# Token and position embedding on one core: the positions loaded in one DMA, two sequences with direct indices, natural order of the gathers

## The chip, the cores and the metric

The kernel runs on one core of a Trainium2 chip. The time is the device time of one execution in microseconds; a comparison uses several runs of each kernel on the same chip. Beside the times there is a profile of one execution, with every engine instruction and every DMA packet.

The engines that matter here: GpSimd (POOL in the profile) issues the gathers, VectorE (DVE) adds, ScalarE (ACT) copies, TensorE (PE) transposes the index table, and SyncE (SP) issues the plain loads and the stores. All transfers run on 16 DMA engines.

## The reference

```python
batch, seq_len, vocab_size, d_model = 32, 512, 50000, 512
def reference(indices, embedding_table, position_embed):
    token_embed = embedding_table[indices]
    return (token_embed + position_embed).astype(np.float32)
```

Indices are 64-bit when they reach the chip (32 x 512 of them), the table is 50,000 rows of 512 float32 (2 KB a row), the positions are 512 rows of 2 KB (1 MB), and the output is 32 x 512 rows of 2 KB (33.55 MB). So 33.55 MB of rows are gathered, the same number of bytes is stored, and 1 MB of positions and 0.14 MB of indices are loaded beside them.

## The kernel before

A sequence has 512 = 128 x 4 rows. Partition p holds rows 4p to 4p+3 of a sequence; the four are called k = 0 to 3. One gather fetches one k of one sequence b: 128 rows, one per partition, 256 KB, into the slot of that sequence. There are 23 slots in SBUF (`slots`), each for a whole sequence, so that sequence 23 takes the slot of sequence 0 again. In all there are 32 x 4 = 128 gathers, 128 adds (`tensor_tensor`, one per gather) and 68 stores, most of them of two k at once (512 KB, 4 KB a partition).

Nothing is scheduled by a planner: each engine's instructions are written out in order, with semaphores between them. The list `order` (lines 73 to 75) gives the order of gathers on POOL and of adds on VectorE, which is the same; the list `stores` (76 to 81) gives the stores on SP. A gather is numbered g by its place in `order`, from 0. Before, the first 16 gathers run in two halves: k = 0 and 1 of the first four sequences (`FIRST = 4`), then k = 2 and 3 of the same four; the rest goes sequence by sequence.

The gathers need an index per partition. For the first `FIRST` sequences the indices are loaded directly (`idx0`, lines 105 and 109), with 32 B pieces: sequence 0 in one DMA, sequences 1 to 3 in a second. For the others the whole index array is loaded in long rows (`idx_raw`, line 113), cast to float (164), transposed on TensorE in four steps (154), and cast back into `idx_t` by four VectorE casts (170). These casts stand on VectorE between the adds of gathers, at places that `g == 7` (the first cast) and `g == 9` (the last four) set. POOL waits for `idx_t` before gather `FIRST * K`, which is gather 16 (line 133).

The positions come in four DMAs of 256 KB, one per k (`load_pos`, line 98), on SP: k = 0 and k = 1 among the index loads, k = 2 when k = 1 has landed (116), k = 3 when the first gather has landed (118). ScalarE copies each k from `pos_sb` in SBUF to `pos_ps` in PSUM (182), and all 128 adds read `pos_ps`; in sequence 0 an add waits for the copy of its k (174).

On SP the stores (191) stand behind the loads; each waits for the count of adds it needs. On POOL a gather g waits for gather g - 16 to have landed (148), and the first gather of a sequence from 23 on waits for the stores of the slot's last user (137).

Of the kernel before, what the change touches and what calls it, by code (L numbers as in the profile page):

```python
# [8 lines left out]
K = 4  # L9
SLOTS = 23  # L10
LANES = 16
FIRST = 4
Q = 32


# [1 line left out]
def kernel(  # L17
# [64 lines left out]

    sem = tc.alloc_semaphore
    s_first, s_next, s_raw = sem("s_first"), sem("s_next"), sem("s_raw")
    s_pos = [sem(f"s_pos{k}") for k in range(K)]
# [8 lines left out]
    def rounds(g):  # L94
        return 16 * (g // LANES + 1)

    def load_pos(engine, k):
        engine.dma_start(out=pos_sb[:, k, :], in_=pos_rows[:, k, :]).then_inc(
            s_pos[k], 16
        )  # L100

    with tc.tile_critical(no_gpsimd_drain=True):  # L102


        nc.sync.dma_start(out=idx0[:, 0, :], in_=idx_first[:, 0, :]).then_inc(
            s_first, 16
        )
        load_pos(nc.sync, 0)
        nc.sync.dma_start(out=idx0[:, 1:, :], in_=idx_first[:, 1:, :]).then_inc(
            s_next, 16  # L110
        )
        load_pos(nc.sync, 1)
        nc.sync.dma_start(
            out=idx_raw[:], in_=idx_rows.rearrange("r (s w) -> r s w", w=2)
        ).then_inc(s_raw, 16)
        nc.sync.wait_ge(s_pos[half - 1], 16)
        load_pos(nc.sync, half)
        nc.sync.wait_ge(s_gather[0], 16)
        load_pos(nc.sync, half + 1)


        nc.gpsimd.memset(ones[:], 1.0).then_inc(s_ident, 1)  # L122
# [1 line left out]
            out=ident[:], in_=ones[:], pattern=[[-1, P]],  # L124
# [2 lines left out]
        )._wait_ge(s_ident, 1).then_inc(s_ident, 1)  # L127
        nc.gpsimd.wait_ge(s_first, 16)
        for g, (b, k) in enumerate(order):
            if g == half:  # L130
                nc.gpsimd.wait_ge(s_next, 16)
            if g == FIRST * K:
                nc.gpsimd.wait_ge(s_idx, J)
            if b >= SLOTS and k == 0:
                done = sum(1 for x in stores if x[1] == b - SLOTS)
                nc.gpsimd.wait_ge(s_out[b - SLOTS], 16 * done)
            if b < FIRST:
                where = idx0[:, b, 2 * k : 2 * k + 1]
            else:
                where = idx_t[:, k, b : b + 1]  # L140
            ins = nc.gpsimd.indirect_dma_start(  # L141
                out=slots[b % SLOTS][:, k, :],
                out_offset=None,
                in_=table,
                in_offset=bass.IndirectOffsetOnAxis(ap=where, axis=0),
            ).then_inc(s_gather[g % LANES], 16)
            if g >= LANES:
                ins._wait_ge(s_gather[g % LANES], rounds(g - LANES))
# [11 lines left out]


        for g, (b, k) in enumerate(order):
            if g == 7:
                nc.vector.tensor_copy(  # L164
                    out=idx_f[:].rearrange("r p k -> r (p k)"), in_=idx_raw[:, :, 0]
                )._wait_ge(s_raw, 16).then_inc(s_cast, 1)
            if g == 9:
                nc.vector.wait_ge(s_turn, K)
                for j in range(J):
                    nc.vector.tensor_copy(  # L170
                        out=idx_t[j * Q : (j + 1) * Q, :, :], in_=turned[:, :, :, j]
                    ).then_inc(s_idx, 1)
            if b == 0:
                nc.vector.wait_ge(s_ps, k + 1)
            part = slots[b % SLOTS][:, k, :]
            nc.vector.tensor_tensor(  # L176
                out=part, in0=part, in1=pos_ps[:, k, :], op=add
            )._wait_ge(s_gather[g % LANES], rounds(g)).then_inc(s_add, 1)


        for k in range(K):
            nc.scalar.copy(out=pos_ps[:, k, :], in_=pos_sb[:, k, :])._wait_ge(  # L182
                s_pos[k], 16
            ).then_inc(s_ps, 1)


# [1 line left out]
        for adds, b, at, n in stores:  # L188
# [3 lines left out]
                out=out_rows[b][:, at : at + n, :],  # L192
                in_=slots[b % SLOTS][:, at : at + n, :],
# [32 lines left out]
```

## Time and profile before

| | before |
|---|---|
| median of 5 runs | 183.41 us (183.33 to 183.49) |
| the profiled execution's own time | 183.44 us |
| its span in the profile | 182.2 us |
| POOL busy, instructions | 122.2 us (67%), 134 |
| VectorE busy, instructions | 89.0 us (49%), 133 |
| ScalarE busy | 3.6 us |
| TensorE busy | 1.0 us |
| read from HBM, written to HBM | 34.75 MB, 33.55 MB |
| mean traffic over the span | 375 GB/s |

The span runs from the first to the last recorded event of the program; the time has 1.24 us around it. [...] A DMA share of an engine stretch can be a little above 1, since packets overlap at their ends. A line number (L141) is that of the kernel above. In the timeline, what stands in brackets is the idle time before an instruction and what ended it.

### The profile page before, as it was taken

To read this page: it belongs to the slowest core of one execution; us is meant where nothing else is said; L and a number is where in the kernel's file an instruction comes from. 1 tells how busy PE (TensorE), PEld (TensorE's weight loads), DVE (VectorE), ACT (ScalarE), POOL (GpSimd) and SP (SyncE) were. 2 spreads that over 40 slices of the span, in tenths; PEclk is the share of its full clock that TensorE was granted. 3 is DMA by queue.
4 is the path that set the end of the run, shared out by engine and by line. 5 is a ranking of instruction groups with operands and counts; after the bars stand their busy time and mean duration, and the time that the engine had idled before them with its cause. 6 is when DMAs were issued, how large, how long until landed. Compare 5 with 4: busy or idle time off the path is not lost.

```text
span 182.2 us, 427 instructions
## 1 busy us (share of the span) xinstructions
PE 1.0 (1%) x4; PEld 0.4 (0%) x4; DVE 89.0 (49%) x133; ACT 3.6 (2%) x5; POOL 122.2 (67%) x134
## 2 busy tenths in 40 slices
PE   0002000000000000000000000000000000000000
PEld 0000000000000000000000000000000000000000
DVE  0137646446544455555555545645556555556300
ACT  2220000000000000000000000000000000000000
POOL 4777777777777777777777777777777777760000
DMA  3899999999999999999999999999999999999900
GB/s 99 237 354 369 345 401 397 399 410 413 402 412 415 405 418 418 416 412 406 401 406 416 421 420 418 420 418 417 420 419 419 421 418 420 417 419 418 361 6 0
DMA packets 21299, 68.34 MB, mean 375 GB/s; under 512 B 3760, under 2 KB 3888, under 8 KB 21296
## 3 DMA queue, kind: packets, MB, share of 16 engines
q0 software_dynamic: 10240, 33.56, 47.4%
q1 hardware_dynamic: 11056, 34.76, 47.4%
q14 instruction: 3, 0.02, 0.0%
HBM read 34.75 MB, written 33.55 MB: 375 GB/s over the span
## 4 chain that ended last, share of the span: by engine, by line
POOL 63%; issue 23%; DMA 5%; DVE 2%; POOLq 1%; SPq 0%
POOL slot L141 63%; DMA slot<-in_embedding_table_dram,idx_t 5%; DVE slot L176 2%; DMA idx<-in_indices_dram 1%; POOLq L149 1%; SPq L221 0%; SPq L102 0%
## 5 line engine op out<-in xcount | busy, mean ns | idle before, releaser
L141 POOL DMA_INDIRECT slot<-in_embedding_table_dram,idx_t x112 | 106.2, 948 | 34.1 <-issue 34.1
L176 DVE TENSOR_TENSOR slot<-slot,pos_ps 128x512 f32<-128x512 f32 x128 | 87.8, 688 | 81.9 <-issue 51.0
L141 POOL DMA_INDIRECT slot<-in_embedding_table_dram,idx x16 | 15.4, 960 | 5.9 <-issue 4.6
L182 ACT COPY pos_ps<-pos_sb 128x512 f32<-128x512 f32 x4 | 2.4, 589 | 8.0 <-DMA pos_sb<-in_position_embed_dram 8.0
L182 ACT ACT_TABLE_LOAD x1 | 1.3, 1283 | 1.0 <-SPq L102 1.0
L170 DVE CAST idx_t<-turned 32x128 int32<-32x128 f32 x4 | 1.1, 280 | 0.1
L154 PE MATMUL turned<-ident,idx_f 128*32 128x128 f32 x4 | 1.0, 413 | 16.7 <-issue 16.7
L122 POOL MEMSET ones<- 128x128 f32 x1 | 0.2, 205 | 0.5 <-SPq L102 0.5
L154 PEld LDWEIGHTS turned<-ident,idx_f 128*32 128x32 f32 x4 | 0.4, 131 | 16.8 <-issue 16.7
L123 POOL TENSOR_SCALAR_AFFINE_SELECT ident<-ones 128x128 f32<-128x128 f32 x1 | 0.3, 289 | 0.1
L210 POOL MEMSET const-float32-0.0<- 128x1 f32 x1 | 0.1, 101 | 0.3 <-issue 0.3
L164 DVE CAST idx_f<-idx_raw 128x128 f32<-128x128 int32 x1 | 0.2, 220 | 0.0
L210 POOL MEMSET const-uint8-127<- 128x1 uint8 x1 | 0.1, 118 | 0.0
L210 POOL MEMSET const-bfloat16-1.0<- 128x1 bf16 x1 | 0.1, 112 | 0.0
L210 POOL MEMSET const-float32-1.0<- 128x1 f32 x1 | 0.1, 103 | 0.0
## 6 DMA issues: line engine op xcount, KB each, us to landing
out_dram<-slot SPq DMA_DIRECT2D x60, 512.0 KB
out_dram<-slot SPq DMA_DIRECT2D x8, 256.0 KB
slot<-in_embedding_table_dram,idx_t POOLq DMA_INDIRECT x112
pos_sb<-in_position_embed_dram SPq DMA_DIRECT2D x4, 256.0 KB, 3.0
slot<-in_embedding_table_dram,idx POOLq DMA_INDIRECT x16
idx_raw<-in_indices_dram SPq DMA_DIRECT2D x1, 128.0 KB
idx<-in_indices_dram SPq DMA_DIRECT2D x1, 4.0 KB, 1.6
idx<-in_indices_dram SPq DMA_DIRECT2D x1, 12.0 KB, 3.0
```

What stands on the lines that cost most here:

```text
L122: nc.gpsimd.memset(ones[:], 1.0).then_inc(s_ident, 1)
L123: nc.gpsimd.affine_select(out=ident[:], in_=ones[:], pattern=[[-1, P]], compare_op=mybir.AluOpType.is_equal, fill=0.0, base=0, channel_mul ...
L141: ins = nc.gpsimd.indirect_dma_start(out=slots[b % SLOTS][:, k, :], out_offset=None, in_=table, in_offset=bass.IndirectOffsetOnAxis(ap=whe ...
L149: nc.gpsimd.drain()
L154: ins = nc.tensor.transpose(turned[:, k].rearrange("p b j -> p (b j)"), idx_f[:, :, k], ident[:])
L164: nc.vector.tensor_copy(out=idx_f[:].rearrange("r p k -> r (p k)"), in_=idx_raw[:, :, 0])._wait_ge(s_raw, 16).then_inc(s_cast, 1)
L170: nc.vector.tensor_copy(out=idx_t[j * Q : (j + 1) * Q, :, :], in_=turned[:, :, :, j]).then_inc(s_idx, 1)
L176: nc.vector.tensor_tensor(out=part, in0=part, in1=pos_ps[:, k, :], op=add)._wait_ge(s_gather[g % LANES], rounds(g)).then_inc(s_add, 1)
L182: nc.scalar.copy(out=pos_ps[:, k, :], in_=pos_sb[:, k, :])._wait_ge(s_pos[k], 16).then_inc(s_ps, 1)
L210: nc = _bacc.Bacc("TRN2", target_bir_lowering=False, num_devices=1)
```

## The change

`FIRST` becomes 2, and the indices of these two sequences come in one DMA. The gathers run in natural order, sequence by sequence and k by k. The positions come in one DMA of 1 MB, whose descriptors are 8 KB (all four k of a partition), issued directly after the first indices, with one semaphore. The four adds of sequence 0 read the positions from SBUF (`pos_sb`) and wait for that DMA; all other adds read the copy in PSUM (`pos_ps`), and those of sequence 1 wait for the copies. The index table's first cast now stands before the add of gather 2, its four last casts before the add of gather 4, and POOL waits for the table before gather 8. Only k = 0 and 1 of sequence 0 are stored one by one; those of sequence 1 are stored as a pair.

```diff
-FIRST = 4
+FIRST = 2
...
-    order = [(b, k) for h in range(2) for b in range(FIRST)
-             for k in range(h * half, (h + 1) * half)]
-    order += [(b, k) for b in range(FIRST, B) for k in range(K)]
+    order = [(b, k) for b in range(B) for k in range(K)]
     stores = []
     for g, (b, k) in enumerate(order):
-        if (b <= 1 and k < half) or b == B - 1:
+        if (b == 0 and k < half) or b == B - 1:
...
-        nc.sync.dma_start(out=idx0[:, 0, :], in_=idx_first[:, 0, :]).then_inc(
-            s_first, 16
-        )
-        load_pos(nc.sync, 0)
-        nc.sync.dma_start(out=idx0[:, 1:, :], in_=idx_first[:, 1:, :]).then_inc(
-            s_next, 16
-        )
-        load_pos(nc.sync, 1)
+        nc.sync.dma_start(out=idx0[:], in_=idx_first).then_inc(s_first, 16)
+        nc.sync.dma_start(out=pos_sb[:], in_=pos_rows).then_inc(s_pos, 16)
         nc.sync.dma_start(
             out=idx_raw[:], in_=idx_rows.rearrange("r (s w) -> r s w", w=2)
         ).then_inc(s_raw, 16)
-        nc.sync.wait_ge(s_pos[half - 1], 16)
-        load_pos(nc.sync, half)
-        nc.sync.wait_ge(s_gather[0], 16)
-        load_pos(nc.sync, half + 1)
...
         for g, (b, k) in enumerate(order):
-            if g == half:
-                nc.gpsimd.wait_ge(s_next, 16)
             if g == FIRST * K:
                 nc.gpsimd.wait_ge(s_idx, J)
...
-            if g == 7:
+            if g == 2:
                 nc.vector.tensor_copy(
                     out=idx_f[:].rearrange("r p k -> r (p k)"), in_=idx_raw[:, :, 0]
                 )._wait_ge(s_raw, 16).then_inc(s_cast, 1)
-            if g == 9:
+            if g == 4:
                 nc.vector.wait_ge(s_turn, K)
...
-            if b == 0:
+            if g == 0:
+                nc.vector.wait_ge(s_pos, 16)
+            if b == 1:
                 nc.vector.wait_ge(s_ps, k + 1)
+            pos = pos_sb if b == 0 else pos_ps
             part = slots[b % SLOTS][:, k, :]
             nc.vector.tensor_tensor(
-                out=part, in0=part, in1=pos_ps[:, k, :], op=add
+                out=part, in0=part, in1=pos[:, k, :], op=add
             )._wait_ge(s_gather[g % LANES], rounds(g)).then_inc(s_add, 1)
...
             nc.scalar.copy(out=pos_ps[:, k, :], in_=pos_sb[:, k, :])._wait_ge(
-                s_pos[k], 16
+                s_pos, 16
             ).then_inc(s_ps, 1)
```

More of the change, by code (lines that the diff above doesn't have):

```diff
@@ L83 @@
     sem = tc.alloc_semaphore
-    s_first, s_next, s_raw = sem("s_first"), sem("s_next"), sem("s_raw")
-    s_pos = [sem(f"s_pos{k}") for k in range(K)]
+    s_first, s_raw, s_pos = sem("s_first"), sem("s_raw"), sem("s_pos")
     s_gather = [sem(f"s_gather{n}") for n in range(LANES)]
@@ L95, in rounds @@
         return 16 * (g // LANES + 1)
-    def load_pos(engine, k):
-        engine.dma_start(out=pos_sb[:, k, :], in_=pos_rows[:, k, :]).then_inc(
-            s_pos[k], 16
-        )
     with tc.tile_critical(no_gpsimd_drain=True):
-        nc.sync.dma_start(out=idx0[:, 0, :], in_=idx_first[:, 0, :]).then_inc(
-            s_first, 16
-        )
-        load_pos(nc.sync, 0)
-        nc.sync.dma_start(out=idx0[:, 1:, :], in_=idx_first[:, 1:, :]).then_inc(
-            s_next, 16
-        )
-        load_pos(nc.sync, 1)
+        nc.sync.dma_start(out=idx0[:], in_=idx_first).then_inc(s_first, 16)
+        nc.sync.dma_start(out=pos_sb[:], in_=pos_rows).then_inc(s_pos, 16)
         nc.sync.dma_start(
@@ L182 @@
             nc.scalar.copy(out=pos_ps[:, k, :], in_=pos_sb[:, k, :])._wait_ge(
-                s_pos[k], 16
+                s_pos, 16
             ).then_inc(s_ps, 1)
```

## The prediction

> **What bounds the kernel now.** I read the page first (busy shares, traffic by slice), then the chain of waits, then the timeline of the first 30 us, then busy time and traffic by stretch.
>
> The page, parts 2 and 3:
>
> ```profile
> span 182.2 us, 427 instructions
> ...
> DMA  3899999999999999999999999999999999999900
> ...
> q0 software_dynamic: 10240, 33.56, 47.4%
> q1 hardware_dynamic: 11056, 34.76, 47.4%
> ```
>
> The 16 DMA engines are full from about 9 us to 172 us. Half of that is gathers (q0), half stores plus the small loads (q1). The chain of waits in order of time (start us, us, what) nevertheless names POOL:
>
> ```profile
> 157.19 0.95 POOL slot L141
> 158.14 0.30 issue
> 158.44 8.28 DMA slot<-in_embedding_table_dram,idx_t
> ...
> 170.30 0.69 DVE slot L176
> ```
>
> Both are true. POOL issues a gather every 1.2525 us (0.95 busy, 0.30 issue), from the second gather to the last, whatever the DMA does. Each gather is 262,144 B and calls for a store of the same size, so POOL's pace asks for 2 x 262,144 / 1.2525 = 418.6 GB/s. Traffic by stretch (columns: start:end, length, busy of PE, PEld, DVE, ACT, POOL with counts, clock, DMA share, GB/s):
>
> ```profile
> 0.00:6.00 6.00, 0.00 (x0) 0.00 (x0) 0.00 (x0) 2.32 (x3) 3.18 (x9) 1.00 0.49 155
> 6.00:10.00 4.00, 0.00 (x0) 0.00 (x0) 1.28 (x2) 0.14 (x1) 3.09 (x4) 1.00 0.80 199
> 10.00:14.00 4.00, 0.00 (x0) 0.00 (x0) 1.51 (x4) 1.18 (x2) 3.09 (x4) 1.00 1.02 387
> ...
> 100.00:160.00 60.00, 0.00 (x0) 0.00 (x0) 33.03 (x48) 0.00 (x0) 45.37 (x49) 1.00 1.03 419
> 165.00:170.00 5.00, 0.00 (x0) 0.00 (x0) 2.75 (x4) 0.00 (x0) 0.00 (x0) 1.00 1.02 416
> ```
>
> The full DMA moves 416 to 419 GB/s, which is POOL's demand almost exactly. A backlog built at the start is therefore never worked off. It shows as the time from a gather's issue to its add: 3.6 us for the first (2.91 to 6.51), 6.2 for the seventeenth (23.14 to 29.36), 8.1 for the last (162.21 to 170.30). The end is thus set by bytes: the DMA time lost at the start, plus all bytes at about 418 GB/s, plus a fixed close (last add 170.30, no DMA after 174, span 182.2). By 10 us, 6 x 155 + 4 x 199 = 1,726 KB have moved, worth 4.1 us at 418, so 5.9 us are lost there. That is the stage which the change rebuilds:
>
> ```profile
> 2.91 1.14 POOL L141 DMA_INDIRECT slot<-in_embedding_table_dram,idx  x1 [1.32 <-DMA idx<-in_indices_dram]
> ...
> 6.51 0.69 DVE L176 TENSOR_TENSOR slot<-slot,pos_ps 128x512 f32<-128x512 f32 x1 [6.51 <-DMA slot<-in_embedding_table_dram,idx]
> ...
> 9.41 0.69 DVE L176 TENSOR_TENSOR slot<-slot,pos_ps 128x512 f32<-128x512 f32 x1 [2.21 <-DMA slot<-in_embedding_table_dram,idx]
> ...
> 13.12 0.95 POOL L141 DMA_INDIRECT slot<-in_embedding_table_dram,idx  x1 [0.30 <-issue]
> 13.27 1.34 DVE L176 TENSOR_TENSOR slot<-slot,pos_ps 128x512 f32<-128x512 f32 x2 [0.89 <-DMA slot<-in_embedding_table_dram,idx]
> ...
> 18.62 1.21 DVE L170 CAST idx_t<-turned 32x128 int32<-32x128 f32 x4
> ...
> 23.14 0.95 POOL L141 DMA_INDIRECT slot<-in_embedding_table_dram,idx_t  x1 [0.30 <-issue]
> ```
>
> To be seen: the fourth add starts at 13.27; the index table is ready at 18.62 + 1.21 = 19.83 and first needed at 23.14, a cover of 3.3 us.
>
> [...]
>
> **The change, part by part**, against the profiled 183.44 us (span 182.2 and 1.24 around it; the median of the five runs is 183.41).
>
> *First indices.* One DMA for two sequences, 256 pieces of 32 B, instead of 128. Now it goes from 1.03 to landing in 1.6 us; the 384-piece one takes 3.0 us, but behind position traffic. SP's issue is 0.38 us for the one and 0.43 for the other. An engine gets 8 more pieces, whose packet records last 7 to 9 ns each. So the first gather, and all of POOL's row behind it, starts later by between 0.05 us and 0.5 us (a third of the step 1.6 to 3.0); I take 0.15.
>
> *Positions.* Four DMAs of 256 KB become one, issued at about 1.47 us, where k=0 goes now. Now k=0 and 1 land by about 5.4, k=2 is issued at 5.55 only and k=3 after the first gather landed (6.5), so 0.5 MB run beside the gathers and ahead of the first store in the same queue. After: the 1 MB takes 1,049 KB / 418 = 2.5 us, from about 2.5 to 5.0; with landing 5.3 to 5.9. The first add does not need them before 6.5, so the new wait costs nothing; without that cover it would be 0.6 us. Packet records show 84 ns for 2 KB and 159 for 4 KB, so larger descriptors save an engine only some 0.2 us; I count it within the next sum.
>
> *Traffic moved by 10 us.* Now q1 has moved 1.02 MB (packet records), of which 0.88 MB positions. After: positions complete, +0.17 MB; the first store (issued 7.2, nothing ahead of it) +0.1 to 0.26 MB; gathers, with 0.25 MB less beside them in 7 to 10 us, 0 to +0.22 MB. Sum 0.27 to 0.65 MB, or 0.65 to 1.55 us at 418. I take 0.8: between 6 and 10 us the trace also has gather packets that last 0.5 to 2.1 us instead of 0.16, which will come again and hold stores too. These long packets thin out and are gone after 100 us; they belong to the rows gathered, and those stay.
>
> *Index table.* Sequences read directly: two, not four, so gather 8 waits for idx_t, all later gathers behind it, and every add and store behind these. It starts at 13.12 + 0.15 = 13.27 if nothing holds it. idx_t needs the add of gather 3 (0.69), then four casts (1.21), 0.1 for the signal: on time if that add starts by 11.27. Now it starts at 13.27, behind k=2 and 3 and the first stores. With the second gather landing at 9.4 as now, gathers 2 and 3 (0.52 MB) and part of a store (0.26 MB) take 1.9 us: 11.3 to 11.7, so POOL stands 0 to 0.5 us. Bounds: 0 and 2.0 (no earlier than now). Meanwhile the DMA has stores of gathers 0 to 7 to move (2.1 MB, 5 us), and the lag of 6.2 us against 3.6 says that 2 us of backlog cover POOL's stand. I cost it at nothing; uncovered it is 0.4.
>
> *Adds from SBUF.* Four of 128 change source; 0.69 us each either way ([...] the trace has 688 with PSUM). The four ACT copies (0.59 each) no longer stand before adds 0 to 3; they hid behind landing gathers already. Blocked gathers: 0 to 4 x 0.69 = 2.8 us. I take 0, as POOL has the same cover.
>
> *Order and stores.* One pair of 256 KB stores becomes one of 512 KB: one SP issue (0.34 us) less on a queue that waits for adds. Nothing. SP loses its two waits between loads; nothing is queued there by then but stores.
>
> Sum: -0.8 + 0.15 = -0.65: 182.8 us.
>
> **The rivals.**
>
> *The index wait reaches the end (slower).* Place: POOL before gather 8. Price: the lateness beyond 13.27, 0.4 to 2.0 us, plus 0.15. It decides if the add of gather 3 starts after 11.27 and the lag grows back to its 8.1 us, in which case the end follows POOL's row: 183.44 + 0.15 + 0.4 to 2.0 = 184.0 to 185.6, say 184.3. For it: the lag does grow now, from 6.2 to 8.1 between 23 and 65 us. Against: it then stays flat for 100 us, which says that it is a sum of losses and not a level it is drawn to.
>
> *Gain spent again (same).* With less backlog some engines run dry between 5 and 9 us and while POOL stands; 0.65 us is half the traffic of 1.3 us. 183.4.
>
> *The SBUF port (slower).* Each of the four adds holds a gather, and POOL's later start shows as above: half of 2.8 less the gain, 184.2.
>
> *No effect:* positions were hidden anyway, since POOL's row bounds alone. Then only the 0.15 remains: 183.6.
>
> **How the numbers follow.** A measurement of this kernel tells 0.2% (0.37 us) from no change. Forecast 0.44 (182.8, own range 182.0 to 183.07); same 0.23 (gain spent or no effect); index wait 0.25; port 0.08. Faster 0.44, same 0.23, slower 0.33. From 182.1, where 1.5 us of gain would land, to 184.6, which leaves out the upper half of the index wait and little else, is 8 in 10.
>
> **What would show it.** Right: positions landed by 6 us; above 199 GB/s in 6 to 10 us; the seventeenth gather's lag near 5 us; last add at 169.6. Index wait: a gap in POOL's row before gather 8, of the size of the lateness of the fourth add. Port: gathers over 0.95 us or add gaps in the first 12 us. Wrong above all: a lag of 8 us again at the end, with POOL's row later, or new long packets where the positions are read.

## The result, and the profile after

| | before | after |
|---|---|---|
| median | 183.44 us (183.11 to 183.90, 50 runs) | 183.92 us (183.26 to 184.46, 30 runs) |
| ratio | | 1.0021, 95% interval 1.0015 to 1.0028 |
| profiled execution, span | 183.44, 182.2 us | 183.40, 182.2 us |
| last gather issued, last add started | 162.21, 170.30 us | 162.80, 171.37 us |

The changed kernel is slower, by some 0.4 us. Its 30 times fall into two groups, 183.26 to 183.52 and 183.86 to 184.46; the profiled execution belongs to the first. The two profiled spans are equal, although the last add is 1.07 us later, and the two groups differ less in their spans than in the time outside them. Both are taken up below, in "What the close hides".

The page of the changed kernel, parts 2, 3 and 6 (a DMA issue: what, queue, count, size, us from issue to landing):

```profile
span 182.2 us, 422 instructions
...
DMA  4989999999999999999999999999999999999910
...
q0 software_dynamic: 10240, 33.56, 47.7%
q1 hardware_dynamic: 10208, 34.75, 47.6%
...
pos_sb<-in_position_embed_dram SPq DMA_DIRECT2D x1, 1024.0 KB, 5.4
```

The DMA engines are again full nearly throughout. Note the third digit of the DMA row, an 8 where before had a 9: at 9 to 14 us the engines now have gaps (their share is 0.91 from 10 to 14 us, where it was 1.02). The one position DMA takes 5.4 us from issue to landing.

Traffic by stretch of the changed kernel (columns as in the prediction: start:end, length, busy of PE, PEld, DVE, ACT, POOL, clock, DMA share, GB/s):

```profile
0.00:6.00 6.00, 0.00 (x0) 0.00 (x0) 0.00 (x0) 1.28 (x1) 3.06 (x9) 1.00 0.57 171
6.00:10.00 4.00, 0.43 (x3) 0.31 (x4) 1.82 (x4) 2.14 (x4) 3.09 (x4) 1.00 0.87 305
10.00:14.00 4.00, 0.60 (x3) 0.12 (x1) 2.72 (x7) 0.00 (x0) 3.11 (x3) 1.00 0.91 292
14.00:18.00 4.00, 0.00 (x0) 0.00 (x0) 2.03 (x4) 0.00 (x0) 3.07 (x4) 1.00 0.98 327
18.00:30.00 12.00, 0.00 (x0) 0.00 (x0) 5.82 (x10) 0.00 (x0) 9.21 (x10) 1.00 0.99 349
30.00:60.00 30.00, 0.00 (x0) 0.00 (x0) 15.65 (x23) 0.00 (x0) 22.70 (x24) 1.00 1.02 405
...
100.00:160.00 60.00, 0.00 (x0) 0.00 (x0) 32.56 (x49) 0.00 (x0) 45.40 (x48) 1.00 1.03 417
```

The first two rows show the gain that was forecast: 6 x 171 + 4 x 305 = 2.25 MB by 10 us, where before had 1.73. The next rows show it spent. Before moved 387 GB/s from 10 to 14 us, and after that:

```profile
14.00:18.00 4.00, 1.04 (x4) 0.43 (x4) 2.75 (x5) 0.00 (x0) 2.91 (x4) 1.00 0.98 366
18.00:30.00 12.00, 0.00 (x0) 0.00 (x0) 7.10 (x14) 0.00 (x0) 9.13 (x10) 1.00 1.01 378
```

The changed kernel moves 292, 327 and 349 in these three stretches. By 14 us its lead is 3.41 against 3.27 MB, by 18 us it is gone (4.72 against 4.74), and by 30 us it is 0.36 MB behind. From 100 to 160 us it also runs at 417 GB/s instead of 419: over 60 us that is 0.12 MB, or 0.3 us.

The timeline of its start (start us, us, engine, what; in brackets the idle time before):

```profile
3.02 1.14 POOL L120 DMA_INDIRECT slot<-in_embedding_table_dram,idx  x1 [1.44 <-DMA idx<-in_indices_dram]
...
6.91 2.14 ACT L164 COPY pos_ps<-pos_sb 128x512 f32<-128x512 f32 x4 [4.65 <-DMA pos_sb<-in_position_embed_dram]
...
7.95 1.31 DVE L158 TENSOR_TENSOR slot<-slot,pos_sb 128x512 f32<-128x512 f32 x2 [7.95 <-DMA slot<-in_embedding_table_dram,idx]
8.22 1.25 POOL L120 DMA_INDIRECT slot<-in_embedding_table_dram,idx  x1 [0.30 <-issue]
...
10.96 0.69 DVE L158 TENSOR_TENSOR slot<-slot,pos_sb 128x512 f32<-128x512 f32 x1 [0.47 <-DMA slot<-in_embedding_table_dram,idx]
11.02 1.45 POOL L120 DMA_INDIRECT slot<-in_embedding_table_dram,idx  x1 [0.30 <-issue]
11.57 1.21 DVE L149 CAST idx_t<-turned 32x128 int32<-32x128 f32 x4
...
14.02 0.94 POOL L120 DMA_INDIRECT slot<-in_embedding_table_dram,idx_t  x1 [0.30 <-issue]
...
162.80 0.95 POOL L120 DMA_INDIRECT slot<-in_embedding_table_dram,idx_t  x1 [0.30 <-issue]
...
171.37 0.69 DVE L158 TENSOR_TENSOR slot<-slot,pos_ps 128x512 f32<-128x512 f32 x1 [0.42 <-issue]
```

Two gathers beside adds with two SBUF inputs take 1.25 and 1.45 us instead of 0.95; a third, issued at 9.77 beside the add that starts at 9.74, takes 0.95. With the first gather 0.11 later, gather 8 starts at 14.02 instead of 13.12. It has no index wait: the table was ready at 11.57 + 1.21 = 12.78. At the end, the lag from the last gather to its add is 171.37 - 162.80 = 8.6 us, 8.1 before.

The chain of waits of the changed kernel, around the place where it leaves POOL:

```profile
134.03 0.95 POOL slot L120
134.98 0.30 issue
135.28 7.59 DMA slot<-in_embedding_table_dram,idx_t
...
143.46 0.69 DVE slot L158
```

It has the form of the chain before: POOL's row without a gap, one landing gather of 7.6 us, then adds.

So the last add's 1.07 us are, in these two profiles, 0.59 of a later last gather plus 0.48 of a longer lag. (The 0.90 at gather 8 shrinks to 0.59 because this kernel issues the later gathers every 1.2503 us and the kernel before every 1.2529, a difference that I did not follow up.)

### The profile page after: what moved, and what is told of

It reads as the page before. It is cut to its first block, busy times and chain, and to the rows that moved or that the text cites. A ratio compares the mean times of both kernels' runs of the same rounds, so it can differ in the third digit from the quotient of the medians.

```text
span 182.2 us, 422 instructions
## 1 busy us (share of the span) xinstructions
PE 1.0 (1%) x4; PEld 0.4 (0%) x4; DVE 89.2 (49%) x133; ACT 3.4 (2%) x5; POOL 122.7 (67%) x134
## 4 chain that ended last, share of the span: by engine, by line
POOL 53%; issue 27%; DVE 9%; DMA 5%; SPq 0%
POOL slot L120 53%; DVE slot L158 9%; DMA slot<-in_embedding_table_dram,idx_t 4%; DMA idx<-in_indices_dram 1%; SPq L203 0%; SPq L94 0%
## 5 line engine op out<-in xcount | busy, mean ns | idle before, releaser
L120 POOL DMA_INDIRECT slot<-in_embedding_table_dram,idx_t x120 | 113.5, 946 | 36.6 <-issue 36.6
L158 DVE TENSOR_TENSOR slot<-slot,pos_ps 128x512 f32<-128x512 f32 x124 | 85.1, 687 | 74.2 <-issue 47.0
L120 POOL DMA_INDIRECT slot<-in_embedding_table_dram,idx x8 | 8.6, 1070 | 3.6 <-issue 2.1
L158 DVE TENSOR_TENSOR slot<-slot,pos_sb 128x512 f32<-128x512 f32 x4 | 2.7, 706 | 8.7 <-DMA slot<-in_embedding_table_dram,idx 8.7
```

What stands on the lines that cost most here:

```text
L120: ins = nc.gpsimd.indirect_dma_start(out=slots[b % SLOTS][:, k, :], out_offset=None, in_=table, in_offset=bass.IndirectOffsetOnAxis(ap=whe ...
L158: nc.vector.tensor_tensor(out=part, in0=part, in1=pos[:, k, :], op=add)._wait_ge(s_gather[g % LANES], rounds(g)).then_inc(s_add, 1)
```

## What the experiments ask

Four questions, each with its theories:

- **The body of the run.** The index tile `idx0` shrank from 128 to 64 B a partition, and all tiles behind it moved: slot 0 lies at byte 27904 of a partition before (109 x 256), and at 27840 after. *Placement* says that this alone slows the DMA. *Port* and *descriptors* put the loss at the start: gathers blocked by adds with two SBUF inputs, or the 8 KB pieces. (*Port* is a name: the profiles show which gathers take long and beside which adds, not what the two share.)
- **The close.** Why are the spans equal?
- **The end.** *Bytes*, the prediction's model: time lost by the DMA at the start plus all bytes. *Row* (of POOL's gathers, issued one after another): POOL's last gather plus a lag that settles at about 8 us whatever happened before. *First touch*: long gather packets belong to the rows gathered.
- **The sum.** What remains if POOL's row is kept?

The runs fell on three chips. The kernel before takes 183.4 us on the first, 176.5 and 176.7 in two series on the second, and 176.4 on the third, so each ratio is taken to the kernel before on the same chip in the same series. (For the comparison of before and after the chip is not on record; by its times it is put with the first.)

Last gather, last add, and the lag between them, from the profile of each run; median differences are to the kernel before beside it:

| kernel | chip | gather 8 | last gather | last add | lag | median, us |
|---|---|---|---|---|---|---|
| before | 1 | 13.12 | 162.21 | 170.30 | 8.1 | 0 |
| after | 1 | 14.02 | 162.80 | 171.37 | 8.6 | +0.48 |
| a1_pad | 1 | 13.82 | 162.62 | 170.45 | 7.8 | +0.03 |
| b1_shift | 1 | 13.15 | 162.23 | 170.22 | 8.0 | +0.16 |
| a2_pad_psum | 1 | 13.79 | 162.88 | 170.49 | 7.6 | -0.14 |
| a3_pad_pos4 | 1 | 13.40 | 162.15 | 169.85 | 7.7 | +0.21 |
| t1_late | 2 | 13.09 | 161.85 | 169.25 | 7.4 | +0.35 |
| w1_before_same | 2 | 13.08 | 161.78 | 169.09 | 7.3 | -0.13 |
| w2_pad_same | 2 | 13.35 | 162.11 | 169.36 | 7.3 | +1.30 |
| b2_onepos | 2 | 14.16 | 162.92 | 170.55 | 7.6 | +1.22 |
| p1_pool_later | 2 | 14.20 | 162.99 | 170.96 | 8.0 | +0.99 |
| p2_pool_mid | 3 | 13.16 | 163.45 | 171.46 | 8.0 | +1.34 |
| d1_extra_mb | 2 | 13.09 | 162.01 | 170.01 | 8.0 | +1.11 |
| a1_pad2 | 2 | 13.79 | 162.72 | 170.55 | 7.8 | +1.27 |
| after2 | 2 | 13.28 | 162.19 | 171.16 | 9.0 | +1.62 |
| c1_row_kept | 3 | 13.23 | 162.02 | 169.88 | 7.9 | +0.79 |
| c2_row_kept_shift | 3 | 13.10 | 161.84 | 171.49 | 9.6 | +1.85 |

t1_late differs from the kernel before only after the last store, so up to its last add it is the profile of the kernel before on the second chip. In what follows its 161.85, 169.25 and 7.4 are the base. The third chip has no profile of the kernel before; p2_pool_mid equals it up to gather 63, and there it lies within 0.1 us of t1_late (gather 8 at 13.16 and 13.09). There is one profile of each kernel, and unchanged parts of the row differ by some 0.3 us from one profile to another, so a few tenths in this table are no finding.

## Placement, port and descriptors

**The changed kernel with the tiles where they were (a1_pad).**

```diff
-    idx0 = sbuf("idx0", [P, FIRST, 2 * K], i32)
+    idx0 = sbuf("idx0", [P, 4, 2 * K], i32)
...
-        nc.sync.dma_start(out=idx0[:], in_=idx_first).then_inc(s_first, 16)
+        nc.sync.dma_start(out=idx0[:, 0:FIRST, :], in_=idx_first).then_inc(s_first, 16)
```

> The changed kernel with the tile of the first indices given room for four sequences again (128 B a partition, of which 64 are used), so that positions and slots lie at the addresses that they have in the kernel before (slot 0 at 27904 = 109 x 256 instead of 27840). Theory 'placement': the 64 B shift makes DMA packets of 4 KB last 159 to 174 ns instead of exactly 159, 0.5% of a DMA that is full for 150 us: this run then moves 419 GB/s from 100 to 160 us, all packets there last 159 ns, and the time falls by 0.6 to 0.8 us, to 183.0 to 183.3. Theory 'start': the loss comes from the first 40 us (positions landing at 7.3 us, blocked gathers, more long packets): the time stays at 183.8 to 184.0 and the traffic at 417.

Measured: 183.40 us, ratio 1.0008 (1.0000 to 1.0016). The stretch of its body, the last gather and the last add:

```profile
100.00:160.00 60.00, 0.00 (x0) 0.00 (x0) 32.96 (x48) 0.00 (x0) 45.40 (x48) 1.00 1.03 419
```

```profile
162.62 0.95 POOL L120 DMA_INDIRECT slot<-in_embedding_table_dram,idx_t  x1 [0.30 <-issue]
...
170.45 0.69 DVE L158 TENSOR_TENSOR slot<-slot,pos_ps 128x512 f32<-128x512 f32 x1 [0.40 <-DMA slot<-in_embedding_table_dram,idx_t]
```

419 GB/s are back, and the lag is 7.8. The packet records show it most sharply: from 110 to 160 us every 4 KB store packet lasts 159 ns here and in the kernel before, but in the changed kernel a third of them last longer, up to 173 ns, mean 160.0. By the two ratios the tile shift of 64 B costs 0.13% of the time (their intervals leave 0.03 to 0.23), 0.2 of the 0.4 us; by the medians it is nearly all. The theory had asked for 0.6 to 0.8 us.

Why a slot at 27840 makes store packets longer was not shown. 27904 is a multiple of 256 and 27840 lies 192 past one, and the expectations count from there; but slot 0 was run only at these two places and at 28096, again 192 past one, so the runs don't show that 256 B, or any other step, is what counts. *Aligned* stands below for the places of the kernel before, slot 0 at 27904, and for nothing more.

**The kernel before, with its tiles moved (b1_shift).** 192 B a partition are put ahead of `idx_raw`; slot 0 then lies at 28096.

```diff
+    gap = sbuf("gap", [P, 48], i32)
     idx_raw = sbuf("idx_raw", [P, Q * K, 2], i32)
```

> The kernel before with a tile of 192 B a partition that nothing uses ahead of the index tiles, so that positions and slots begin 192 B past a multiple of 256 B, as in the changed kernel. Theory 'placement': 0.5 to 0.9 us slower than before (183.9 to 184.3), 417 GB/s from 100 to 160 us, and times that scatter more from run to run. Theory 'start': no difference from before (183.4).

Measured: 183.53 us, ratio 1.0022 (1.0010 to 1.0034), store packets of 159 to 173 ns (mean 160.1).

```profile
100.00:160.00 60.00, 0.00 (x0) 0.00 (x0) 33.02 (x48) 0.00 (x0) 45.36 (x49) 1.00 1.03 416
```

With nothing else changed, 416 GB/s instead of 419, and by the ratio as much time as the whole change costs, less than the 0.5 to 0.9 us that were expected. In this one profile the last add is not late (170.22), so the loss is shown by the packets and the 11 times, not by that execution's end.

**Aligned, and no add from SBUF (a2_pad_psum).** a1_pad, and all adds read PSUM.

```diff
-            if g == 0:
-                nc.vector.wait_ge(s_pos, 16)
-            if b == 1:
+            if b == 0:
                 nc.vector.wait_ge(s_ps, k + 1)
-            pos = pos_sb if b == 0 else pos_ps
+            pos = pos_ps
```

> The padded changed kernel with the adds of the first sequence reading the positions from PSUM like all others (each waits for its ACT copy). Theory 'SBUF port': the gathers of 1.25 and 1.45 us at 8.2 and 11.0 us and the step in POOL's row are due to adds with two SBUF inputs: gather 8 starts at 13.2 to 13.5 instead of 14.0; if POOL's row reaches the end the time falls by 0.4 to 0.6 us against the padded kernel, if the backlog covers it the times are equal within 0.15. If other instructions block the gathers (the casts of the index table), their durations stay.

Measured: 183.23 us, ratio 0.9996 (0.9987 to 1.0005): equal to the kernel before. Its timeline around gather 8:

```profile
11.00 0.95 POOL L120 DMA_INDIRECT slot<-in_embedding_table_dram,idx  x1 [0.30 <-issue]
...
12.31 1.21 DVE L149 CAST idx_t<-turned 32x128 int32<-32x128 f32 x4
...
13.79 0.95 POOL L120 DMA_INDIRECT slot<-in_embedding_table_dram,idx_t  x1 [0.59 <-DVE idx_t L149]
```

No gather but the first (1.14) lasts over 1 us. Over all runs the same holds: of the six profiles with adds from SBUF four have such gathers, of the eleven with all adds from PSUM none. So the blocked gathers (1.05 to 1.46 us) go with the adds from SBUF, though not every such add has one; by what way an add holds a gather, no run shows. But in place of the blocked gathers comes the index wait: gather 8 stands 0.59 us (0.30 is its usual issue). With a first gather at 3.29 (3.07 in a1_pad) it starts at 13.79, no better than a1_pad's 13.82.

**Aligned, positions in four DMAs (a3_pad_pos4).** a1_pad, with four 256 KB DMAs back to back in place of the one of 8 KB descriptors.

```diff
+        for k in range(K):
+            nc.sync.dma_start(out=pos_sb[:, k, :], in_=pos_rows[:, k, :]).then_inc(
+                s_pos, 16
+            )
```

> The padded changed kernel with the positions in four DMAs of 256 KB, issued one directly after another, in place of one with 8 KB descriptors. Theory 'large descriptors': the first 8 KB packets last 1.2 us each and hold the gathers behind them; with 2 KB packets the positions land by 6.5 us and the first gather by 7.0 instead of 7.9; the time is 0 to 0.4 us below the padded kernel. Rival: the amount loaded early is what counts, whatever the packets: positions and first gather land as late as with one DMA, and the times are equal within 0.15.

Measured: 183.58 us, ratio 1.0017 (1.0009 to 1.0025). Its first add starts at 8.39, later than the changed kernel's 7.95, and its positions have landed at 7.34 instead of 6.91: the large descriptors aren't what delays the start. The end of its timeline:

```profile
162.15 0.95 POOL L123 DMA_INDIRECT slot<-in_embedding_table_dram,idx_t  x1 [0.30 <-issue]
...
169.85 0.69 DVE L161 TENSOR_TENSOR slot<-slot,pos_ps 128x512 f32<-128x512 f32 x1 [0.42 <-issue]
```

Here POOL's row lost little, and the last add is 0.6 us earlier than in a1_pad. Yet its median is 0.18 higher, and its profiled span 0.1 longer. So on this chip an earlier end of the work isn't always an earlier end of the program.

## What the close hides

From SyncE's release (all stores landed) to the span's end, the six profiles of the first chip show 7.2 to 9.0 us:

| | before | after | a1 | b1 | a2 | a3 |
|---|---|---|---|---|---|---|
| release, us | 174.11 | 174.96 | 174.09 | 173.77 | 174.30 | 173.35 |
| span, us | 182.2 | 182.2 | 182.3 | 182.3 | 182.5 | 182.4 |

Releases that lie 1.6 us apart end within 0.3 us of each other. Most of SyncE's closing instructions that take time last 0.70 or 1.40 us on this chip (1.40, 0.70, 0.70, 0.70 and 0.69 in before; 1.21, 1.40 and 0.69 in after). That the close waits for something that comes in steps, so that a lateness below one step is swallowed, is a guess from these figures; no run shows what it waits for.

The two groups of times are another step, and it lies outside the span. For each of these executions both the time and the span are known. On the first chip they differ by 1.2 to 1.3 us or by 1.7 to 1.8, with nothing between; on the other two chips always by 1.7 to 1.8. All times in the changed kernel's upper group have the larger difference, 21 of its 32 executions in all, against 2 of 48 of the kernel before in the series of a1_pad. The mean spans are 182.27 and 182.15 us. So some 0.1 of the 0.4 us lies in the span, and the rest is how often this outer step is taken. It is taken in 4 of 11 executions of b1_shift, 3 of 22 of a1_pad, 1 of 14 of a3_pad_pos4 and none of 14 of a2_pad_psum: more often with the tiles moved. What the step is, no run shows. The size of a cost on this chip is therefore not the size of the delay in the work.

**A late step alone (t1_late).** The kernel before, with one small ScalarE copy between the last store's landing and the end.

```diff
-        nc.sync.wait_ge(s_rest, 16 * rest)
+        nc.scalar.copy(out=ident[:], in_=ones[:])._wait_ge(
+            s_rest, 16 * rest
+        ).then_inc(s_late, 1)
+        nc.sync.wait_ge(s_late, 1)
```

> The kernel before with one ACT copy of 128 x 128 (about 0.3 us, 0.4 with its signals) between the landing of the last store and SyncE's leaving of the body; nothing else moves. Theory 'steps': what follows the body runs on SyncE in steps of 0.7 us, so times come in groups 0.6 to 0.7 us apart: the runs stay at 183.3 to 183.5 or go to 183.9 to 184.1, few between. Theory 'straight': every run is 0.3 to 0.4 us longer, 183.75 in the median with the same narrow spread.

Measured: 176.88 us beside 176.53, ratio 1.0033 (1.0016 to 1.0050). The copy lasts 0.30 us, and its lateness appears in full and without groups. But this run fell on the second chip, where the close lasts 1.6 to 1.9 us and has no steps. So both kinds of step stay an observation of the first chip; they could not be switched on or off.

The second and third chip show a smaller difference. Kernels that keep SyncE's loads of before close in 1.55 to 1.58 us; a1_pad2, after2, w2, b2, c1 and c2 in 1.87 to 1.91, and in these an 8 KB packet of the queue that the profile calls "instruction" falls behind the release. (On the first chip it lies behind it in after, at 176.69 with the release at 174.96, and ahead of it in before, at 173.49 with 174.11.) This was seen, not tested.

## What sets the end

**Gathers of the same rows (w1_before_same, w2_pad_same).** All gathers take the rows of the first two sequences, so the output differs; w1 is the kernel before with that edit, w2 is a1_pad with it.

```diff
-            if b < FIRST:
-                where = idx0[:, b, 2 * k : 2 * k + 1]
-            else:
-                where = idx_t[:, k, b : b + 1]
+            where = idx0[:, b % 2, 2 * k : 2 * k + 1]
```

> The kernel before, but every gather reads the rows of the first or second sequence again (1,024 rows of the table instead of 16,384; the output is then not the reference's; the index table is still made and waited for). Theory 'first touch': the gather packets that last 0.4 to 2 us instead of 0.16 come from rows read for the first time and are gone after the first 16 gathers (23 us): the DMA time lost falls by 2 to 3 us after 20 us, the lag of the last gather from 8.1 to under 6 us, the last store has landed by 172 us instead of 174.1. Rival 'load': they come from gathers and stores running together while queues fill; the same rows change nothing.

> The padded changed kernel with the same edit: all gathers read the rows of the first two sequences again. If long packets are what took back the traffic gained by 10 us (theory 'first touch'), then here the work ends (last store landed) earlier than in the kernel before with the same edit by the predicted 0.4 to 0.8 us, or, with the backlog gone, as much later as POOL's row is late (0.4 to 0.7 us). If something else takes it back, it ends as in that kernel within 0.2 us although POOL's row is late.

Measured: w1 176.40 us, ratio 0.9992 (0.9977 to 1.0007), with 68 gather packets over 0.4 us, where the kernel before has 63 on this chip (t1_late) and 80 on the first. Rows touched again and again give the same long packets; they don't belong to the rows, and *first touch* falls. w2 has 81 such packets and 177.83 us, ratio 1.0090 (1.0058 to 1.0121). Its profiled execution is its fastest (176.66), so the profile doesn't show where the others lose. Its tiles are aligned and its profiled row is 0.3 us late, so about 1 us of that difference stays open.

**One position DMA alone (b2_onepos).** The kernel before, its order and index loads kept, with the 1 MB DMA right after the first indices.

```diff
-        load_pos(nc.sync, 0)
+        nc.sync.dma_start(out=pos_sb[:], in_=pos_rows).then_inc(s_pos[0], 16)
...
-        load_pos(nc.sync, 1)
...
-        nc.sync.wait_ge(s_pos[half - 1], 16)
-        load_pos(nc.sync, half)
-        nc.sync.wait_ge(s_gather[0], 16)
-        load_pos(nc.sync, half + 1)
...
```

> The kernel before with one part of the change: the positions in one DMA of 8 KB descriptors directly after the first indices; order, direct indices, stores and adds stay, and the addresses too. Theory 'traffic' of the prediction: 0.3 to 0.7 us less DMA time lost by 20 us, the last store landed 0.3 to 0.7 us before 174.1, the time 182.8 to 183.4. Rival 'given back': by 10 us more is moved, by 30 us the gain is gone in longer packets, the last store lands at 174.1 within 0.2. Rival 'late first gathers': the sequence behind the large DMA starts 1 us later and the time is 183.6 to 184.0.

Measured: 177.75 us, ratio 1.0075 (1.0047 to 1.0103). Its row:

```profile
4.34 0.95 POOL L131 DMA_INDIRECT slot<-in_embedding_table_dram,idx  x1 [0.30 <-issue]
6.66 0.94 POOL L131 DMA_INDIRECT slot<-in_embedding_table_dram,idx  x1 [1.38 <-DMA idx<-in_indices_dram]
...
162.92 0.94 POOL L131 DMA_INDIRECT slot<-in_embedding_table_dram,idx_t  x1 [0.30 <-issue]
```

The rest of the direct indices (12 KB) is now issued behind the megabyte and takes 4.5 us from issue to landing, 3.0 in the kernel before, and the third gather waits 1.38 us for it. By 10 us the DMA has moved 6 x 188 + 4 x 274 = 2.22 MB and lost 4.7 us at 418 GB/s, where t1_late with 154 and 234 GB/s has lost 5.6, so *bytes* as the prediction used it would have it faster. The row is 1.07 us later, and that is what arrives: last add +1.3, median +1.2.

**A later row alone, at the start and in the middle (p1_pool_later, p2_pool_mid).** The kernel before, with two memsets on POOL into a slot that is not yet used, ahead of the first gather (p1, whose edit is shown) or, under `if g == 64`, ahead of gather 64 (p2).

```diff
+        nc.gpsimd.memset(slots[SLOTS - 1][:, 0, :], 0.0).then_inc(s_hold, 1)
+        nc.gpsimd.memset(slots[SLOTS - 1][:, 1, :], 0.0).then_inc(s_hold, 1)
+        nc.gpsimd.wait_ge(s_hold, 2)
         for g, (b, k) in enumerate(order):
```

> The kernel before with two memsets of 128 x 512 on POOL (into the last slot, which is free until gather 88) between the first indices and the first gather: POOL's row starts about 1 us later, everything else is as before. Theory 'row' (now mine): the last add comes a settled lag of 7.3 to 8.3 us after the last gather's issue, whatever happened at the start, so the end moves with POOL's row: last add, last landing and time later by the delay, within 0.3 us. Theory 'bytes' (the prediction's): the DMA has a backlog of 2 us that covers the delay, and the end moves by 0 to 0.3 us.

> The kernel before with the two memsets (1.1 us of POOL) ahead of gather 64 instead of ahead of the first. Theory 'row' in its strong form (the lag is a level to which the queues return at any time): lag 8 again at the end, last add and time 0.8 to 1.2 us later. Weaker form (the lag is built up in the first 40 us, while queues are short, and then only kept): the lag falls by the 1.1 us at gather 64 and stays there, the end moves by 0 to 0.3 us.

Measured: p1 177.65 us, ratio 1.0055 (1.0040 to 1.0071); p2 177.72 us, ratio 1.0057 (1.0037 to 1.0077). The end of t1_late, the base, then three lines of p1:

```profile
161.85 0.94 POOL L141 DMA_INDIRECT slot<-in_embedding_table_dram,idx_t  x1 [0.30 <-issue]
...
169.25 0.69 DVE L176 TENSOR_TENSOR slot<-slot,pos_ps 128x512 f32<-128x512 f32 x1 [0.42 <-DMA slot<-in_embedding_table_dram,idx_t]
```

```profile
4.01 1.14 POOL L144 DMA_INDIRECT slot<-in_embedding_table_dram,idx  x1 [0.29 <-POOL slot L130]
...
162.99 0.95 POOL L144 DMA_INDIRECT slot<-in_embedding_table_dram,idx_t  x1 [0.30 <-issue]
...
170.96 0.69 DVE L179 TENSOR_TENSOR slot<-slot,pos_ps 128x512 f32<-128x512 f32 x1 [0.57 <-DMA slot<-in_embedding_table_dram,idx_t]
```

The timeline of p2:

```profile
82.90 0.54 POOL L135 MEMSET slot<- 128x512 f32 x1
...
84.68 0.95 POOL L145 DMA_INDIRECT slot<-in_embedding_table_dram,idx_t  x1 [0.77 <-POOL slot L136]
...
163.45 0.94 POOL L145 DMA_INDIRECT slot<-in_embedding_table_dram,idx_t  x1 [0.30 <-issue]
...
171.46 0.69 DVE L180 TENSOR_TENSOR slot<-slot,pos_ps 128x512 f32<-128x512 f32 x1 [0.72 <-DMA slot<-in_embedding_table_dram,idx_t]
```

p1's first gather starts 1.11 us later, its last 1.14, and its median is 0.99 higher: one to one, as *row* says. In the profiled execution the last add is even 1.71 later, because the lag is 8.0 instead of 7.4, which *row* did not expect. But p1 alone doesn't decide between the theories. At the first gather no backlog stands that could cover the delay: by 14 us p1 has moved 2.92 MB where t1_late has 3.22, and 0.3 MB at 418 GB/s are 0.7 us, so a sum of early losses asks for most of the delay too.

p2 decides. With a lag of 8.5 us, so some 8 us of backlog in the queues, POOL stands for 1.5 us (84.68 where 83.20 was due), while the DMA goes on at 420 GB/s and loses nothing. The lag drops from 8.5 us at gather 63 to 7.1 at gather 64 and 6.8 at gather 72, as it must if the DMA works on meanwhile. By gather 90 it is back at 8.0, then it is between 7.3 and 8.1 and ends at 8.0. Of the 1.5 us of delay most arrives at the end, as the strong form of *row* expected: 1.0 us by the ratio, 1.3 by the medians. Long packets return: 1.1 us of extra time per engine from 100 to 160 us, where the kernel before has none, and the traffic there is 410 GB/s instead of 419. So in this run the DMA loses time after its queues have become shorter.

**More bytes at the start (d1_extra_mb).** The kernel before, with one more load of 1 MB into a slot that is not yet used, on SyncE ahead of the first store (gather 88, which takes that slot, waits for it).

```diff
+        nc.sync.dma_start(
+            out=slots[SLOTS - 1][:], in_=embedding_table[0 : P * K].rearrange("(p k) d -> p k d", k=K)
+        ).then_inc(s_hold, 16)
```

> The kernel before with one more DMA of 1 MB (512 table rows into the last slot, which is free until gather 88) on SyncE ahead of the first store, about 2.5 us of work for all DMA engines at 8 to 11 us; POOL's row is not touched. Theory 'row': once queues have settled the lag is that of before; the last add moves by less than 0.8 us. Theory 'bytes': the end moves by the 2.5 us that the DMA needs for it, and the lag of the last gather is 10.6 us.

Measured: 177.77 us, ratio 1.0061 (1.0030 to 1.0092). One stretch of t1_late, then of d1_extra_mb:

```profile
20.00:30.00 10.00, 0.00 (x0) 0.00 (x0) 6.00 (x13) 0.00 (x0) 7.56 (x9) 1.00 1.01 379
```

```profile
20.00:30.00 10.00, 0.39 (x2) 0.00 (x0) 6.53 (x13) 0.00 (x0) 7.56 (x9) 1.00 1.03 420
```

*Bytes* asks for 1,049 KB / 418 = 2.5 us; the median rises by 1.1 (0.5 to 1.6 by the interval of the ratio). The difference is won back here: with a megabyte more waiting, the engines run at 420 GB/s at once instead of 379, and there are 24 long packets instead of 63. The profiled execution is the fastest of the nine; in it the last add is 0.8 us later, 0.16 by the row and 0.6 by the lag, 8.0 instead of 7.4. *Row* in its strict form (nothing at all) is missed by that. The aligned runs of the second and third chip end with lags of 7.3 to 8.0, and I can't say what places a run in that interval.

## The sum on the chips with a short close

**The changed kernel and its aligned form again (after2, a1_pad2).** The kernels are those of after and a1_pad, run beside p1 and d1.

> The changed kernel once more, beside the others of this call. Both theories of the end expect it later than before by what its POOL row is late (0.9 us at gather 8) and what its placement costs (0.3 to 0.5 us) as long as nothing after the body hides it: 1.0 to 1.5 us where SyncE's close takes 1.5 us, 0.3 to 0.6 us where it takes 7 to 9 us in steps.

> The changed kernel with the padded index tile once more. Theory 'row': 0.7 to 1.0 us later than before with a short close (its POOL row is 0.5 to 0.7 us late), 0 to 0.3 with the long one; in either case earlier than the changed kernel by 0.3 to 0.6 us.

Measured: after2 178.28 us, ratio 1.0086 (1.0053 to 1.0120); a1_pad2 177.93 us, ratio 1.0065 (1.0042 to 1.0088). Here the close is short, and the change costs 1.5 us. In after2's profile no gather is blocked and gather 8 waits only 0.05 us for the table; its row is 0.3 late. Its lag at the end is 9.0 and still growing (7.8 at gather 48). a1_pad2 has blocked gathers of 1.11 and 1.38 us, a row 0.9 late and a lag of 7.8. So of the two profiles of the changed kernel one has blocked gathers, and both have the moved tiles. The intervals of the two ratios overlap widely, so the 0.4 us between these two kernels are not clear of the noise.

**The row kept (c1_row_kept), and the same with the tiles moved (c2_row_kept_shift).** c1 has the single position DMA and the natural order, but four sequences of direct indices, loaded in two DMAs ahead of the positions, the casts at their old places, all adds from PSUM, and slot 0 at 27904. c2 adds the 192 B of b1_shift. (The lines shown are against the kernel before; the last one is in c2 only.)

```diff
-    order = [(b, k) for h in range(2) for b in range(FIRST)
-             for k in range(h * half, (h + 1) * half)]
-    order += [(b, k) for b in range(FIRST, B) for k in range(K)]
+    order = [(b, k) for b in range(B) for k in range(K)]
...
+        nc.sync.dma_start(out=idx0[:, 0, :], in_=idx_first[:, 0, :]).then_inc(s_first, 16)
+        nc.sync.dma_start(out=idx0[:, 1:, :], in_=idx_first[:, 1:, :]).then_inc(s_next, 16)
+        nc.sync.dma_start(out=pos_sb[:], in_=pos_rows).then_inc(s_pos, 16)
...
+    gap = sbuf("gap", [P, 48], i32)
```

> The changed kernel with what delays POOL's row and what shifts the addresses taken back, and the rest kept (positions in one DMA of 8 KB descriptors, natural order, its stores): four direct sequences, their indices in two DMAs ahead of the positions, the table's casts where they were, all adds from PSUM, slots at 27904. Theory 'row': gather 0 at 2.9 us and gather 8 at 13.0 to 13.2 as in the kernel before, lag at the end 7.3 to 8.3, and the time equals that of before within 0.2%. Rival 'positions': the single large DMA and the later first adds cost by themselves: last add and time 0.6 us or more after before's, although the row is on time.

> The kernel of the run above with 192 B a partition that nothing uses ahead of the index tiles, so that slots and positions begin 192 B past a multiple of 256 B as in the changed kernel. Theory 'placement': packets of 4 KB last 159 to 174 ns, lag of the last gather 0.4 to 1.0 us more than in the run above, time 0.3 to 0.9 us more. Otherwise equal within 0.2.

Measured: c1 177.17 us, ratio 1.0038 (1.0019 to 1.0057); c2 178.23 us, ratio 1.0086 (1.0055 to 1.0117). The end of c1, then of c2:

```profile
162.02 0.95 POOL L124 DMA_INDIRECT slot<-in_embedding_table_dram,idx_t  x1 [0.30 <-issue]
...
169.88 0.69 DVE L160 TENSOR_TENSOR slot<-slot,pos_ps 128x512 f32<-128x512 f32 x1 [0.43 <-DMA slot<-in_embedding_table_dram,idx_t]
```

```profile
161.84 0.95 POOL L125 DMA_INDIRECT slot<-in_embedding_table_dram,idx_t  x1 [0.30 <-issue]
...
171.49 0.69 DVE L161 TENSOR_TENSOR slot<-slot,pos_ps 128x512 f32<-128x512 f32 x1 [0.60 <-DMA slot<-in_embedding_table_dram,idx_t]
```

c2's last gather is issued 0.18 us earlier than c1's and its last add starts 1.61 us later: the lag has grown to 9.6 (8.5 at gather 48, 9.2 at gather 96). That is placement alone, 0.48% of the time or about 0.85 us (0.2 to 1.5 by the intervals), clear of the noise and more than on the first chip. c1 itself misses the expectation of *row*, by about 0.5 us. Its 0.67 us (by the ratio; 0.79 by the medians) and its last add, 0.63 after t1_late's, are what the rival *positions* of that run asked for. 0.3 of it lie in the longer close and about 0.1 in the first gather; up to 0.4 stay open, and a cost of the single position DMA by itself is not excluded.

So the 1.5 us are, as far as these runs go, made of placement (0.85 from c1 against c2, the difference that is clear of the noise), POOL's row (0.3 to 0.9 in the profiles), the close (0.3) and a rest that is open. The intervals are 0.6 us wide and more, and a finer split would be more than they bear. No version tried that computes the same output beats the kernel before; a2_pad_psum equals it.

## Why the prediction was wrong

It forecast 182.8 us and faster; the result is 183.92 and slower.

- **First indices, +0.15: right.** The first gather starts at 3.02 instead of 2.91.
- **Positions land by 5.3 to 5.9: wrong by 1 us.** They landed at 6.9. The sum took 1 MB at the full rate from 2.5 us on. In the packet records the first 8 KB packet of each of the 16 engines lasts 0.85 to 1.34 us, where 84 ns for 2 KB would give 0.34. But in a3_pad_pos4, whose 2 KB packets last at most 0.77, the positions land later still, so why a megabyte takes this long at the start stays open. Packets of the first gather start only at 6.3 (5.1 before), and the first add at 7.95 instead of 6.51. The cover named for this wait had been the landing of gather 0, and that moved too.
- **Traffic moved by 10 us, +0.27 to 0.65 MB: right.** It was 0.52.
- **What that traffic is worth, 0.8 us: wrong, and this is the step that failed.** The working took the loss after 10 us as the same before and after, since it read the flat lag as "a sum of losses and not a level it is drawn to". It is not the same. Packet records added up to 170 us give 67.32 MB before and 66.86 after: 0.45 MB less, which at 418 GB/s is the 1.07 us of the last add. After was 0.52 MB ahead at 10 us, so it lost 0.97 MB between 10 and 170 us, 0.89 of it by 30. p2 shows such a loss caused on purpose: with 8 us of backlog, most of a delay of POOL's row arrives at the end, and the lag comes back after it was cut. d1 shows the other side: of a megabyte in the queues more than half is paid back by the median, since the DMA loses less time while they are full (420 GB/s from 20 to 30 us instead of 379). With aligned tiles the end follows POOL's last gather plus a lag of 7.3 to 8.1 us. A lag that stays flat while supply and demand are both 418 GB/s can't tell a stored loss from a level; only a disturbance can.
- **The long packets "belong to the rows gathered": wrong.** w1 gathers the same rows over and over and has them still (68, and 63 in t1_late); d1 has few (24). In p2 and d1 they go with short queues. Why a packet then lasts 0.4 to 2 us was not measured.
- **Index table, 0 to 0.5 us of standing: right in size,** and of no weight in after. It is 0 in after, 0.05 in after2, 0.29 in a2_pad_psum.
- **Adds from SBUF, 0 taken of 0 to 2.8 us: wrong by 0.8 us of POOL's row in after's profile,** 0.3 and 0.5 in two gathers. That such an add can hold a gather, and by how much, was the author's estimate; the trace of before shows no such add. The adds themselves take 691 to 748 ns from SBUF and 687 from PSUM in after, so "0.69 us each either way", an estimate for SBUF, nearly held. "POOL has the same cover" fails with the lag: in p2 1.0 to 1.3 of 1.5 us came through 8 us of backlog. Not every execution has these stalls.
- **Not in the prediction at all: the 64 B.** `FIRST` sizes a tile, the tile moves its successors, and slot 0 went from 27904 to 27840. The diff shows it only through the shape of `idx0`. By the ratios it costs 0.2 of the 0.4 us on the first chip.
- **The close** was taken as fixed. On the first chip it lasts 7.2 us in after's profile and 8.1 in before's, so that a last add 1.07 us later left the span as it was.

Of the rivals, "gain spent again" happened by 18 us, and the port's blocked gathers happened, for 0.8. The index wait's rival named the right condition, that the lag grows back and the end follows POOL's row; its own wait hardly occurred. "No effect" had the mechanism in one clause, "POOL's row bounds alone", but its 183.6 leaves out the blocked gathers and the 64 B.

## What to carry to other kernels

Where an issuing engine asks for as much as the DMA moves (here 418.6 GB/s, and 416 to 419), disturb one of them before deciding which sets the end: a delay of some 1 us in the middle of the loop, where the queues are full, shows whether there is slack (in p2, of 1.5 us, 1.0 to 1.3 came through). When an edit changes the size of any tile, compare the base addresses of the large DMA targets before and after: here a move of the slots by 64 or 192 B cost 0.13 to 0.48% of the time. Judge a small change by the last work, the span and the time together: here the close hid most of a microsecond, and a step of 0.5 us lay outside the span.

## What the hardware showed that I had not expected

- SBUF slots at byte 27840, 64 B below their place in the kernel before, or 192 B above it: 33 to 39% of the 4 KB store packets last longer than 159 ns, up to 180 (0 to 2% with slots at 27904), 416 to 417 GB/s instead of 418 to 419 in kernels alike but for this, and 0.13 to 0.48% of the time.
- A lag of some 8 us from a gather's issue to its add that comes back after it was cut to 6.8 (p2), with gather packets of 0.4 us and more while it is shorter.
- The close: 8.1 us for the kernel before on the first chip, 1.6 for programs with the same loads on the two others; most of the 7 us between its medians there. And a step of 0.5 us outside the span, taken on the first chip in some executions only.
- First 8 KB packets of a 1 MB load that last 0.85 to 1.34 us, and no packet of the gather that was issued at 3.02 before 6.3 us, when the load is nearly through (6.5).
